# A Mamba-2 and short-convolution decode step on one core: VectorE's instructions go into written order through the scan

## Chip, core and metric

The kernel runs as one program on one core of a Trainium2 chip. The metric is the device time of one execution in microseconds. Three executions of the kernel before took 1029.29, 1029.47 and 1030.23 us, with a median of 1029.47 us. A further execution was taken with a profile; it took 1030.42 us, and the span of its instructions, from the first to the last, is 1028.60 us.

## The reference

One layer of a decoder trunk, for 256 prompt tokens and 8 sample sequences of 8 tokens each (320 columns in all), with a model width of 2048. All in float32:

```python
h = rmsnorm(x, norm_w)
proj = einsum('bld,de->ble', h, w_in)          # 2048 -> 13344 columns
z_s, xbc, dt_raw, z_c, b_c, c_c, v_c = split(proj)
xbc = silu(causal_dwconv(xbc, state, w4) + bias)      # x, B, C: width-4 convolution
xs, bm, cm = split(xbc)
dt = softplus(dt_raw + dt_bias);  a = -exp(a_log)
y_s, h_new = ssd_scan(xs, dt, a, bm, cm, d_skip, h0)  # 32 heads x 64, state 128, 4 groups
y_s = grouped_rmsnorm(y_s * silu(z_s), ssd_norm_w, 4)
conv_out = causal_dwconv(c_c * v_c, state2, w3)
y_c = b_c * conv_out * silu(z_c)
out = rmsnorm(x + concat(y_s, y_c) @ w_out, final_norm_w)
```

The scan works on chunks of 128 tokens. Inside a chunk, with the running sum `a_cum` of `dt * a`, it forms `decay = exp(min(a_cum[l] - a_cum[s], 0))` under a causal mask, `cb = C B^T`, and `y = (cb * decay) @ (x * dt)` for each head; between chunks it carries a state `h` of 64 x 128 for each head. The outputs are the two token groups' results and all new states.

## The kernel before

Everything is laid out with channels on the 128 partitions and the 320 tokens along the free dimension. The input projection is a loop over 104 weight tiles (`tiles`, made by `schedule()`, L82): each gives 128 output channels, as 16 steps over the contraction, each of three matmuls of 128 x 320. Three, because a float32 product is made out of high and low parts: `wh` and `wl` are the parts of the weights, `xh` and `xl` those of the input (`product`, L169). The order of the tiles is by group g = 0 to 3: `B`, `C`, (two short-convolution sets for g = 0), four `x`, four `z`, then one short-convolution set `sc`, `sv`, `sz`, `sb` (two for g = 3); nine more such sets follow. The output projection (16 tiles of two halves) comes last.

**Weights.** `load(i)` (L135) fetches a tile by two DMAs of 512 KB on SP's queue into three half buffers. `split(i)` (L163) cuts a tile into four quarters of 128 x 512: ScalarE casts the quarter to `wh` (L159), VectorE subtracts it from the raw weights and gets `wl` (L160). There are six buffers of a quarter for each, so the casts of quarters 2 and 3 of the next tile wait until TensorE has gone through quarters 0 and 1 of the tile in work. The loop (L793) writes, for tile i: load of i+2, split of i+1, the product of i, and then what is done with its result.

**What is done with a result.** `conv` (L500) for x, B and C: VectorE scales it out of PSUM into a padded tile, GpSimd puts in the old state and keeps the new one, ScalarE makes the first tap (L513), VectorE the other three (L515), ScalarE the SiLU (L518, L521). `short` (L745) is the like for the short convolution, with two taps on VectorE (L763). A `z` tile is scaled by VectorE (L821) and goes through SiLU on ScalarE. Tiles 0 to 5 (B0, C0 and the first short set) are made ahead of the loop, the first four of them in other PSUM tiles.

**The scan rides along.** `decays` (L414) makes the softplus, the running sums and the decay factors; `ssd_group` (L523) is the scan of one group. Both are Python generators, queued in `gens`; within each product, ahead of steps 5, 10 and 15 (`TICKS`), `advance(1)` runs the front one to its next `yield`. So the group's matmuls are spread among those of the projection, a part at a time. The group of z tiles starts its scan after tile z0 (L818); its first part stands at the first tick of z1, three parts to a tile. In the counting used below, part 1 has the transposes of B (L586), part 2 the product `cb` (L599), part 3 the samples' transposes of x (L610), part 5 the first chunk's transposes (L627) and out of them `xdt` and `xw` on VectorE (L629, L632), part 7 the state product `st` of the first chunk (L642, it reads `xw`), part 8 the second chunk's transposes, part 10 its `st`, part 11 the products with the old states, `py` and `up` (L656, L668). `rpart` (L553) makes one of five parts of the decay matrix: VectorE subtracts and clips (L570: four or eight instructions), ScalarE takes the exponential (L573), VectorE multiplies by the masked `cb` (L574). The updates of the old states are a product on GpSimd (L672) and an addition on VectorE (L679), and go out by DMAs on GpSimd's queue (L680).

**Who sets the order.** TensorE's instructions run as they are written (L182). The order on VectorE, ScalarE, GpSimd and SP is made by a planner when the program is built: it walks the written program with costs of its own, and an engine takes, at each planned instant, the first written one of the instructions that are then ready. On the chip each engine runs its list in that order, and an instruction whose input is late holds all that are behind it. Only in the tail, from L935, is VectorE's order the written one too. All small PSUM tiles of the scan share four buffers (`sm`, L111).

## Time and profile before

| | |
|---|---|
| median of three executions | 1029.47 us (1029.29 to 1030.23) |
| profiled execution | 1030.42 us, its span 1028.60 us |
| TensorE busy in the span | 1018.8 us (99%) |
| VectorE, ScalarE, GpSimd busy | 667.5, 492.6, 190.6 us |
| weight low parts on VectorE (L160) | 518 instructions, 365.4 us |
| weight casts on ScalarE (L159) | 518 instructions, 315.5 us |

The profile is of one execution. Its views give, for an engine and a line of the kernel, how long it was busy, and what ended the idle time ahead of an instruction; the timeline gives the start and the duration of single instructions, in us from the start of the span, and merges neighbours of the same line ("x4"). Instructions of one engine overlap at their ends, so the distance from one start to the next is shorter than the duration. A busy time of TensorE is taken from modelled ends, so its waits are seen best in the distance between the starts of two matmuls.

### The profile page before, as it was taken

What the parts mean: (1) busy time and instruction counts of PE and PEld (TensorE: products, weight loads), DVE (VectorE), ACT (ScalarE), POOL (GpSimd) and SP (SyncE); (2) the same over time, 40 slices, a digit from 0 to 9 for tenths busy, and PEclk for the clock granted to TensorE, in tenths of its full rate; (3) what the DMA queues carried; (4) which work ended last, traced back from release to release, by engine and by line L of the source; (5) the groups of instructions that cost most, each with busy time, mean ns of one, the idle gap of its engine ahead of it and who ended that gap; (6) DMA issues with size and microseconds to landing.
All of it is one profiled execution on the core that took longest, in us unless ns stands there. A gap on an engine that the chain in (4) does not pass through costs nothing.

```text
span 1028.6 us, 18694 instructions
## 1 busy us (share of the span) xinstructions
PE 1018.8 (99%) x7233; PEld 997.9 (97%) x7233; DVE 667.5 (65%) x1217; ACT 492.6 (48%) x891; POOL 190.6 (19%) x293
## 2 busy tenths in 40 slices
PE   9999999999999999999999999999999999999997
PEld 9999999999999989999999999999999999999996
DVE  7787758886878777886868555555556544444444
ACT  8456434573457445654445433433345544444450
POOL 0222034210622134213422101111111000000000
PEclk9999999999999999999999999999999999999999
DMA  9354475546473566447546444444445744444412
GB/s 370 118 158 164 143 256 176 177 152 216 165 230 119 193 225 205 144 160 264 180 149 244 163 144 148 160 144 146 154 152 155 256 153 145 150 156 146 148 38 103
DMA packets 63304, 176.62 MB, mean 172 GB/s; under 512 B 10496, under 2 KB 20352, under 8 KB 63088
## 3 DMA queue, kind: packets, MB, share of 16 engines
q1 hardware_dynamic: 59712, 164.98, 48.3%
q0 software_dynamic: 3072, 9.96, 2.7%
q8 instruction: 56, 0.92, 0.4%
q10 hardware_dynamic: 432, 0.49, 0.1%
q14 instruction: 32, 0.26, 0.1%
HBM read 162.83 MB, written 12.58 MB: 171 GB/s over the span
## 4 chain that ended last, share of the span: by engine, by line
PE 88%; DVE 5%; DMA 2%; issue 2%; POOL 1%; ACT 1%; DVEq 0%; POOLq 0%; SPq 0%; ACTq 0%
PE pj L176 20%; PE pj L175 20%; PE pj L177 20%; PE po L175 7%; PE po L176 7%; PE po L177 7%; PE pf L282 3%; DMA R<-acd 2%; POOL ht L672 1%; DVE wl L160 1%; PE pd L699 1%; DVE ht L679 1%; DVE R L570 1%; PE pt L926 1%; DVE R L574 1%
## 5 line engine op out<-in xcount | busy, mean ns | idle before, releaser
L160 DVE TENSOR_TENSOR wl<-wr,wh 128x512 fp32r<-128x512 f32 x518 | 365.4, 712 | 271.3 <-ACT wh L159 267.7
L159 ACT CAST wh<-wr 128x512 fp32r<-128x512 f32 x518 | 315.5, 618 | 393.1 <-PE pj L177 233.8
L175 PE MATMUL pj<-xh,wh 128*128 128x320 f32 x1600 | 501.8, 314 | 0.0
L176 PE MATMUL pj<-xh,wl 128*128 128x320 f32 x1600 | 494.8, 309 | 1.6 <-DVE wl L160 1.6
L177 PE MATMUL pj<-xl,wh 128*128 128x320 f32 x1600 | 494.3, 309 | 0.0
L175 PEld LDWEIGHTS pj<-xh,wh 128*128 128x128 f32 x1600 | 300.6, 188 | 6.0 <-issue 5.4
L176 PEld LDWEIGHTS pj<-xh,wl 128*128 128x128 f32 x1600 | 300.7, 188 | 5.2 <-DVE wl L160 3.0
L177 PEld LDWEIGHTS pj<-xl,wh 128*128 128x128 f32 x1600 | 300.6, 188 | 0.0
L175 PE MATMUL po<-ysh,wh 128*128 128x320 f32 (+1 forms) x256 | 78.3, 306 | 0.0
L176 PE MATMUL po<-ysh,wl 128*128 128x320 f32 (+1 forms) x256 | 78.3, 306 | 0.0
L177 PE MATMUL po<-ysl,wh 128*128 128x320 f32 (+1 forms) x256 | 78.3, 306 | 0.0
L175 PE MATMUL po<-ych,wh 128*128 128x320 f32 (+1 forms) x256 | 78.1, 305 | 0.0
L176 PE MATMUL po<-ych,wl 128*128 128x320 f32 (+1 forms) x256 | 78.1, 305 | 0.0
L177 PE MATMUL po<-ycl,wh 128*128 128x320 f32 (+1 forms) x256 | 78.0, 305 | 0.0
L177 PEld LDWEIGHTS po<-ysl,wh 128*128 128x128 f32 x256 | 48.1, 188 | 0.0
L175 PEld LDWEIGHTS po<-ysh,wh 128*128 128x128 f32 x256 | 48.1, 188 | 0.0
L176 PEld LDWEIGHTS po<-ysh,wl 128*128 128x128 f32 x256 | 48.1, 188 | 0.0
L176 PEld LDWEIGHTS po<-ych,wl 128*128 128x128 f32 x256 | 48.1, 188 | 0.0
L175 PEld LDWEIGHTS po<-ych,wh 128*128 128x128 f32 x256 | 48.0, 188 | 0.0
L177 PEld LDWEIGHTS po<-ycl,wh 128*128 128x128 f32 x256 | 48.0, 188 | 0.0
L902 POOL TENSOR_TENSOR acco<-acco,sqo 128x320 f32<-128x320 f32 x13 | 11.5, 881 | 186.7 <-ACT sqo L898 186.7
L515 DVE SCALAR_TENSOR_TENSOR cv<-pad,vec,cv 128x344 f32<-128x344 f32 x72 | 40.7, 570 | 2.7 <-ACT cv L513 1.6
(254 smaller groups left out, 899.4 us busy)
## 6 DMA issues: line engine op xcount, KB each, us to landing
wr<-in_w_in SPq DMA_DIRECT2D x200, 512.0 KB, 3.5
wr<-in_w_out SPq DMA_DIRECT2D x59, 512.0 KB, 3.7
ht<-in_h SPq DMA_DIRECT2D x32, 256.0 KB, 5.0
out_hs<-ht POOLq DMA_DIRECT2D x32, 256.0 KB, 3.0
R<-acd SPq DMA_DIRECT2D x20, 256.0 KB, 6.3
xw<-in_xw SPq DMA_DIRECT2D x6, 848.0 KB, 10.7
wk<-in_w_out SPq DMA_DIRECT2D x5, 512.0 KB, 6.6
resp<-in_xp SPq DMA_DIRECT2D x1, 2048.0 KB, 9.6
```

The source lines that it names most:

```text
L159: S.copy(h, r)
L160: V.tensor_sub(l, r, h.bitcast(F32))
L175: PE.matmul(ps, h, hi(k), start=start and k == 0, stop=False)
L176: PE.matmul(ps, l, hi(k), start=False, stop=False)
L177: PE.matmul(ps, h, lo(k), start=False, stop=stop and k == KT - 1)
L282: PE.matmul(ps0[i], w[:, i * P:(i + 1) * P], x[:, k, :], start=k == 0 and w is h and x is xh, stop=k == KT - 1 and w is l)
L515: V.scalar_tensor_tensor(out=a, in0=pad[:, k:k + CW], scalar=vec[:, w + k:w + k + 1], in1=a, op0=ALU.mult, op1=ALU.add)
L570: V.tensor_scalar(out=R[:, h, :], in0=R[:, h, :], scalar1=ac_tok[:, c, at:at + 1], scalar2=0.0, op0=ALU.subtract, op1=ALU.min)
L574: V.tensor_tensor(out=R, in0=R, in1=bc(CBm[:, o:o + n].rearrange("p (u l) -> p u l", u=1), [P, nh, n]), op=ALU.mult)
L672: GP.tensor_tensor(out=heads(ht, g), in0=heads(ht, g), in1=decay(b, g), op=ALU.mult)
L679: V.tensor_tensor(out=ht, in0=ht, in1=ups[j], op=ALU.add)
L902: GP.tensor_tensor(out=acc, in0=acc, in1=sq, op=ALU.add)
```

## The change

Four things, all in the order of work; no arithmetic is added or taken out.

1. From the product of tile 6 to the last tile of the scan, VectorE's instructions run as they are written (`manual_schedule` for DVE, closed when short set 6 is through).
2. In the written text, what VectorE makes out of a result of ScalarE or GpSimd is put behind one more `yield`: for the generators of the scan it then stands in the next part, for `conv` and `short` (now generators too, driven by `take` and `finish`) it stands behind the split of the next tile. The number of parts of the scan, and the part in which each matmul stands, are kept: other yields are taken out (`rpart` carries its own, and the wait loop of `decays` goes from 11 to 9).
3. B0 and C0 are no longer worked on ahead of tile 6, but after tile 6 and after tile 7.
4. In the group's norm the reciprocal goes into tile `b` in place of `v`, the tile that ScalarE's square root reads.

```diff
--- before.py
+++ after.py
@@ -423,6 +423,7 @@
         V.tensor_scalar(out=v, in0=v, scalar1=hv[:, 0:1], scalar2=None, op0=ALU.add)
         V.scalar_tensor_tensor(out=nv_, in0=v, scalar=-1.0, in1=v, op0=ALU.mult, op1=ALU.min)
         S.activation(u, nv, AF.Exp)
+        yield
         an = cp.tile([H, 1], F32, name="an")
         V.tensor_copy(an, u[:H, TQ:])
         u = u[:, :TQ]
@@ -461,9 +462,10 @@
         GP.tensor_copy(tot[:, :NB], win(ac, TP + NL - 1, (NL, NB)))
         GP.tensor_copy(tot[:, NB:], ac[:, TP - 1:TP])
         GP.dma_start(totd, tot)
+        yield
         V.tensor_tensor(out=wT[:, :T], in0=wx, in1=dtT[:, :T], op=ALU.mult)
         pad_samples(GP, stk)
-        for _ in range(11):
+        for _ in range(9):
             yield
         SP.dma_start(dec, bc(totd.rearrange("(u h) b -> u (h b)", u=1), [P, H * (NB + 1)]))
         p = sm("tr")
@@ -511,6 +513,7 @@
         a = tp.tile([P, CW], F32, name=f"cv{idx}", tag="cv")
         w = V_CW + 4 * idx
         S.mul(a, pad[:, 0:CW], vec[:, w:w + 1])
+        yield
         for k in range(1, 4):
             V.scalar_tensor_tensor(out=a, in0=pad[:, k:k + CW], scalar=vec[:, w + k:w + k + 1],
                                    in1=a, op0=ALU.mult, op1=ALU.add)
@@ -571,6 +574,7 @@
                                 scalar1=ac_tok[:, c, at:at + 1], scalar2=0.0,
                                 op0=ALU.subtract, op1=ALU.min)
             S.activation(R, R, AF.Exp)
+            yield
             V.tensor_tensor(out=R, in0=R,
                             in1=bc(CBm[:, o:o + n].rearrange("p (u l) -> p u l", u=1), [P, nh, n]),
                             op=ALU.mult)
@@ -590,9 +594,10 @@
         Bst = ssd.tile([P, 2, 2, P], F32R, name=f"Bst{g}", tag="Bst")
         for q in range(2):
             S.activation(Bst[:, q, 0, :], p[:, 2 * P:3 * P], AF.Copy, scale=mq[q])
+        yield
+        for q in range(2):
             V.scalar_tensor_tensor(out=Bst[:, q, 1, :], in0=p[:, 2 * P:3 * P], scalar=mq[q],
                                    in1=Bst[:, q, 0, :].bitcast(F32), op0=ALU.mult, op1=ALU.subtract)
-        yield
         p = sm(f"cb{g}")
         CBm = ssd.tile([P, T], F32, name=f"CBm{g}", tag="CBm")
         for c, (o, n, _) in enumerate(CH):
@@ -615,10 +620,9 @@
         xh_ = t5("xh2", F32R)
         S.activation(xh_, xw, AF.Copy, scale=sgn)
         xst = ssd.tile([P, 512], F32R, name=f"xst{g}", tag="xst")
+        yield
         V.scalar_tensor_tensor(out=xst, in0=xw, scalar=m1, in1=xh_.bitcast(F32), op0=ALU.mult, op1=ALU.add)
-        yield
-        rpart(0)
-        yield
+        yield from rpart(0)
 
         h1 = tl("h1")
         for c in range(2):
@@ -633,8 +637,9 @@
                             in1=perhead(w_tok[:, c, hs]), op=ALU.mult)
             yield
             if c == 0:
-                rpart(1)
-            yield
+                yield from rpart(1)
+            else:
+                yield
             if c == 0:
                 for b in range(4):
                     hload(2 * b)
@@ -642,13 +647,14 @@
             PE.matmul(p, Btok[:, c * P:(c + 1) * P], xw, start=True, stop=True)
             if c == 0:
                 S.copy(h1, p)
+                yield
             else:
                 hf = t5("hf")
                 GP.tensor_tensor(out=heads(hf, g), in0=heads(h1, g),
                                  in1=decay(NB, g), op=ALU.mult)
+                yield
                 V.tensor_tensor(out=hf, in0=hf, in1=p, op=ALU.add)
                 GP.dma_start(O["hp"][g], hf)
-            yield
 
         py = pss.tile([P, 512], F32, name=f"py{g}", tag="py", bufs=1)
         for q in range(2):
@@ -685,8 +691,7 @@
         V.tensor_tensor(out=xdt[2], in0=xdt[2], in1=py, op=ALU.add)
         yield
         for n_ in range(2, len(PARTS)):
-            rpart(n_)
-            yield
+            yield from rpart(n_)
             yield
         yield
         acc = ssd.tile([P, T], F32, name=f"acc{g}", tag="acc")
@@ -727,11 +732,11 @@
         V.tensor_scalar(out=v, in0=p[:, :T], scalar1=1.0 / (4 * P), scalar2=EPS,
                         op0=ALU.mult, op1=ALU.add)
         S.activation(a, v, AF.Sqrt)
-        V.reciprocal(v, v)
-        yield
-        V.tensor_tensor(out=v, in0=v, in1=a, op=ALU.mult)
-        V.scalar_tensor_tensor(out=b, in0=v, scalar=-0.5, in1=a, op0=ALU.mult, op1=ALU.mult)
-        V.scalar_tensor_tensor(out=b, in0=b, scalar=1.5, in1=v, op0=ALU.add, op1=ALU.mult)
+        V.reciprocal(b, v)
+        yield
+        V.tensor_tensor(out=b, in0=b, in1=a, op=ALU.mult)
+        V.scalar_tensor_tensor(out=v, in0=b, scalar=-0.5, in1=a, op0=ALU.mult, op1=ALU.mult)
+        V.scalar_tensor_tensor(out=b, in0=v, scalar=1.5, in1=b, op0=ALU.add, op1=ALU.mult)
         yield
         for j in range(4):
             ct = 4 * g + j
@@ -759,10 +764,11 @@
             a = tp.tile([P, SC], F32, name=f"sa{j}", tag="cv")
             w = V_SW + 3 * j
             S.mul(a, pad[:, 0:SC], vec[:, w:w + 1])
+            held["a"] = a
+            yield
             for k in range(1, 3):
                 V.scalar_tensor_tensor(out=a, in0=pad[:, k:k + SC], scalar=vec[:, w + k:w + k + 1],
                                        in1=a, op0=ALU.mult, op1=ALU.add)
-            held["a"] = a
         elif kind == "sz":
             a = held.pop("a")
             z = tp.tile([P, T], F32, name=f"sz{j}", tag="sz")
@@ -783,6 +789,7 @@
             V.tensor_tensor(out=y, in0=ps, in1=z, op=ALU.mult)
             if j >= NE:
                 S.copy(ych[:, j, :], y)
+                yield
                 V.tensor_sub(ycl[:, j, :], y, ych[:, j, :].bitcast(F32))
                 GP.tensor_copy(ycs[:, j, :], y[:, TP:])
 
@@ -790,41 +797,72 @@
     gens.append(decays())
     group = {}
 
-    for i in [*range(2, NFIRST + NAHEAD), 0, 1, *range(NFIRST + NAHEAD, nin)]:
+    def result(i, ps):
+
+        nonlocal zs
         kind, idx = tiles[i]
-        if i < NFIRST:
-            ps = ps0[i]
-        elif i in ahead:
-            ps = ahead.pop(i)
-        else:
-            load(i + 2)
-            split(i + 1)
-            ps = inproj(i)
         if kind in "BC":
             t = ssd.tile([P, T + P], F32, name=f"{kind}{idx}", tag=kind, bufs=2)
-            conv(ps, ((16 if kind == "B" else 20) + idx, i), t)
+            group[kind] = t
+            yield from conv(ps, ((16 if kind == "B" else 20) + idx, i), t)
             if kind == "B":
                 pad_samples(GP, t)
-            group[kind] = t
         elif kind == "x":
             t = ssd.tile([P, T + P], F32, name=f"x{idx}", tag="xs", bufs=6)
-            conv(ps, (idx, i), t)
+            group.setdefault("x", []).append(t)
+            yield from conv(ps, (idx, i), t)
             pad_samples(GP, t)
-            group.setdefault("x", []).append(t)
         elif kind == "z":
             if idx % 4 == 0:
-                advance(1000)
                 zs = []
                 gens.append(ssd_group(idx // 4, group["B"], group["C"], group["x"], zs))
-                group = {}
+                group.clear()
             z = ssd.tile([P, T], F32, name=f"z{idx}", tag="z", bufs=4)
             V.tensor_tensor(out=z, in0=ps, in1=rb, op=ALU.mult)
             S.activation(z, z, AF.Silu)
             zs.append(z)
         else:
-            short(kind, idx, ps)
+            yield from short(kind, idx, ps)
+
+    zs = None
+    late = []
+
+    def finish():
+        while late:
+            for _ in late.pop(0):
+                pass
+
+    def take(i, ps):
+        if tiles[i][0] == "z" and tiles[i][1] % 4 == 0:
+            advance(1000)
+        gen = result(i, ps)
+        if next(gen, late) is not late:
+            late.append(gen)
+
+    written = ExitStack()
+    for i in range(2, NFIRST + NAHEAD):
+        take(i, ps0[i] if i < NFIRST else ahead.pop(i))
+        finish()
+    first = [0, 1]
+    for i in range(NFIRST + NAHEAD, nin):
+        kind, idx = tiles[i]
+        load(i + 2)
+        split(i + 1)
+        finish()
+        if i == NFIRST + NAHEAD:
+
+            written.enter_context(tc.manual_schedule(engines={mybir.EngineType.DVE}))
+        ps = inproj(i)
+        take(i, ps)
+        if first:
+            finish()
+            n = first.pop(0)
+            take(n, ps0[n])
+        if kind[0] == "s":
             if idx == NE - 1 and kind == "sb":
+                finish()
                 advance(1000)
+                written.close()
                 sst_.close()
                 fp = ctx.enter_context(tc.tile_pool(name="fin", bufs=1, reuse_waits="tile"))
                 ych = fp.tile([P, NSH, T], F32R, name="ych")
@@ -835,6 +873,7 @@
                     S.copy(ych[:, n, :], early[:, n, :])
                     V.tensor_sub(ycl[:, n, :], early[:, n, :], ych[:, n, :].bitcast(F32))
                 GP.dma_start(O["cs"], cso)
+    finish()
     GP.dma_start(O["ss"], sso)
 
 
```

## The prediction

> **What bounds the kernel now.** I read the page's busy times first, then the waits of TensorE's weight loads (PEld), then the timeline around the longest of them.

> ```profile
> span 1028.6 us, 18694 instructions
> PE 1018.8 (99%) x7233; PEld 997.9 (97%) x7233; DVE 667.5 (65%) x1217; ACT 492.6 (48%) x891; POOL 190.6 (19%) x293
> ```
> ```profile
> PEld pj L176 <- DVE wl L160: 3.0, 5, 0.8
> ```
> ```profile
> 227.00:337.00 110.00, 109.59 (x791) 105.13 (x790) 85.92 (x162) 57.74 (x104) 32.10 (x46) 1.00 0.55 184
> ```

> TensorE is the bound. All that another order on VectorE can win is the time in which TensorE waits for VectorE's `wl` in the scan: five waits, 3.0 us, 0.29% of the run. The last row is the second group's 110 us (columns: length, then busy us of PE, PEld, DVE, ACT and POOL, the granted clock, the DMA share): the clock is full, and a group's 42 parts (14 tiles of three) are 2.6 us apart. About 0.2% (2.06 us) is what a measurement of this kernel can tell from no change. So the change has to keep over two thirds of those 3.0 us to be seen as faster.

> ```profile
> 170.33 0.31 PE L175 MATMUL pj<-xh,wh 128*128 128x320 f32 x1
> 171.18 0.41 PE L176 MATMUL pj<-xh,wl 128*128 128x320 f32 x1 [0.55 <-DVE wl L160]
> ```
> ```profile
> 166.78 0.69 DVE L679 TENSOR_TENSOR ht<-ht,up 128x512 f32<-128x512 f32 x1 [0.52 <-POOL ht L672]
> ...
> 170.44 1.29 DVE L160 TENSOR_TENSOR wl<-wr,wh 128x512 fp32r<-128x512 f32 x2
> ```
> ```profile
> 165.69 4.11 POOL L672 TENSOR_TENSOR ht<-ht,dec 128x512 f32<-128x512 f32 x4
> ```

> The reader is to see the cause in these rows: the planner put four state additions (L679) ahead of a `wl`; GpSimd takes 4.11 us for their four factors, each addition waits for its own, and the `wl` behind them comes at 170.44, its matmul 0.85 us after the one before it.

> **What the change removes.** In written order those additions stand two and three parts behind GpSimd's products, and the `wl` of the next tile stand ahead of them. The wait in that place goes in every group, four of the five; the fifth is of the same kind, a `wl` behind scan work, and I count it in: -3.0 us, and no more can be won. Nothing is late next in that place: GpSimd's 4.11 us end before the second part behind, 5.2 us on, and the next use of the additions, the PSUM for the second four `up`, is five parts behind the first. The later additions move `out_hs` on GpSimd's queue, and with it the release of the buffers into which SP's queue loads the next `R`; these are used six parts after the second four `up`. The loads on SP's queue keep their parts. The reciprocal (L730) no longer waits for the square root; no matmul of the scan reads its result. These edits I put at 0, covered by parts of the group in which TensorE needs nothing of VectorE.

> **What it adds: VectorE stops where it could have gone on.** Before a group's `xst` (part 4) stand, in written order, the four `wl` of the next tile, and the last of them waits for TensorE's own progress. What follows in VectorE's queue is, one behind the other: `xst`, eight subtractions of `rpart(0)`, [ScalarE's exponential], the product with `cb`, `xdt`, `xw`. TensorE's `st` in part 7 needs that `xw`. Before, the planner had made the whole `rpart(0)` a tile of x earlier. The rows of the first group:

> ```profile
> 126.96 0.62 ACT L159 CAST wh<-wr 128x512 fp32r<-128x512 f32 x1 [1.15 <-PE pj L177]
> 129.15 0.62 ACT L159 CAST wh<-wr 128x512 fp32r<-128x512 f32 x1 [1.57 <-PE pj L177]
> ```
> ```profile
> 91.59 1.31 DVE L570 TENSOR_SCALAR R<-R,ac_tok 128x64 f32<-128x64 f32 x7
> 124.72 0.75 DVE L618 SCALAR_TENSOR_TENSOR xst<-xw,con,xh 128x512 fp32r<-128x512 f32 x1
> 127.62 0.69 DVE L160 TENSOR_TENSOR wl<-wr,wh 128x512 fp32r<-128x512 f32 x1 [0.94 <-ACT wh L159]
> 128.23 0.69 DVE L629 TENSOR_TENSOR xdt<-xt,dt_tok 128x512 f32<-128x512 f32 x1
> 128.84 0.68 DVE L632 TENSOR_TENSOR xw<-xt,w_tok 128x512 f32<-128x512 f32 x1
> ```
> ```profile
> 150.46 1.28 ACT L562 ACT_TABLE_LOAD   x1 [6.20 <-DMA out_hp<-hf]
> 151.75 0.63 ACT L562 ACTIVATE CE<-R 128x512 f32<-128x512 f32 x1
> 165.95 1.28 ACT L770 ACT_TABLE_LOAD   x1
> 172.16 0.47 ACT L770 ACTIVATE sz<-sz 128x320 f32<-128x320 f32 x1 [4.93 <-DVE sz L769]
> ```
> ```profile
> 132.87 1.02 PE L642 MATMUL st<-xw,Btok 128*128 128x512 f32 x2
> ```

> The last `wl` of tile z3 starts at 127.62, since its cast is let go by TensorE at 126.96 and so is the same under the change. A 128x512 instruction takes the engine 0.61 us from start to start (128.23 to 128.84). `xst` then starts at 128.23 and takes 0.75 at the most; seven subtractions take 1.31, eight 1.5: they end at about 130.4. The exponential is 0.63. ScalarE's last function was the SiLU of z1, so it loads a table first, 1.28 us. The rows at 165.95 and 172.16 show that such a load runs ahead of the data that its function waits for, as far as ScalarE's own list lets it. Two ends, then. If the load is through by 130.4: exponential to 131.1, product 131.7, `xdt` 132.3, `xw` to 133.0, and with 0.05 to reach TensorE (ScalarE's end at 127.58 to VectorE's start at 127.62 is 0.04) 133.1, 0.25 us after 132.87. If the cast at 129.15, which is ready before the exponential and so stands ahead of it in a list made by readiness, comes first: cast to 129.77, load to 131.07, exponential to 131.7, product 132.3, `xdt` 132.95, `xw` to 133.64, at TensorE 133.7: a wait of 0.82 us. I take 0.82, because that cast is ready 1.2 us before the subtractions are done. Four groups: +3.3 us (bounds +1.0 and +3.3).

> [...]

> **A second new wait, at `up`.** The addition that ends `hf` (L649) moves from part 10 to part 11, behind a `wl` that waits for TensorE, and its PSUM buffer is one of the four that `up` of part 11 takes.

> ```profile
> 144.29 0.69 DVE L160 TENSOR_TENSOR wl<-wr,wh 128x512 fp32r<-128x512 f32 x1 [1.26 <-ACT wh L159]
> ```
> ```profile
> 145.35 0.74 PE L668 MATMUL up<-xst,Bst 32*128 32x512 f32 x8
> ```

> The addition can start at 144.29 + 0.61 = 144.90 and ends at 145.59; the fourth `up` begins at most 0.28 us (three eighths of 0.74) behind 145.35. With the 0.05 that is a wait of 0 to 0.29 us for each group; I take the middle, 0.15: +0.6 us (0 to 1.2). Behind the waiting addition on VectorE only part 13 is queued, and `out_hp` on GpSimd's queue goes 3 us later, which nobody waits for.

> **The start of the region.** B0 and C0 move behind tiles 6 and 7; their GpSimd copies and ScalarE's taps and SiLUs go with them. Now a SiLU of B0 lies between the two exponentials of `decays`, so another table load. VectorE's chain in tile 7, behind the last `wl` of tile 8: three taps of B0, parts 4 and 5 of `decays`, an exponential, `wT`, the scaling of `sv`, its taps, the scaling of C0, then the first `wl` of tile 9.

> ```profile
> 50.01 2.53 DVE L515 SCALAR_TENSOR_TENSOR cv<-pad,vec,cv 128x344 f32<-128x344 f32 x5 [0.72 <-ACT cv L513]
> 62.55 0.96 DVE L447 SCALAR_TENSOR_TENSOR stk<-v,q 32x80 f32<-32x80 f32 x4
> 64.14 0.37 DVE L450 TENSOR_SCALAR la<-stk,an 32x320 f32<-32x320 f32 x1
> 64.55 0.81 DVE L453 TENSOR_TENSOR_SCAN ac<-seg,la 32x320 f32<-32x320 f32 x1
> 65.29 0.79 DVE L456 TENSOR_TENSOR_SCAN wx<-la,ges 32x320 f32<-32x320 f32 x1
> 66.69 0.49 DVE L464 TENSOR_TENSOR stk<-wx,stk 32x320 f32<-32x320 f32 x1
> 67.21 0.42 DVE L754 TENSOR_TENSOR pad<-pj,c 128x256 f32<-128x256 f32 x1
> 67.56 0.21 DVE L756 TENSOR_TENSOR pad<-pj,c 128x64 f32<-128x64 f32 x1
> 68.48 1.17 DVE L763 SCALAR_TENSOR_TENSOR sa<-pad,vec,sa 128x336 f32<-128x336 f32 x2
> ```
> ```profile
> 61.78 0.62 ACT L159 CAST wh<-wr 128x512 fp32r<-128x512 f32 x1 [1.14 <-PE pj L177]
> 67.86 0.58 ACT L761 ACTIVATE sa<-pad,vec 128x336 f32<-128x336 f32 x1 [0.77 <-DVE pad L756]
> ```
> ```profile
> 72.28 0.31 PE L176 MATMUL pj<-xh,wl 128*128 128x320 f32 x1
> ```

> The last cast of tile 8 is let go by TensorE at 61.78, its `wl` is through by 63.05. Taps 1.5 (five in 2.53), parts 4 and 5 0.96 + 0.37 + 0.81 + 0.79 = 2.9: 67.5. The exponential, bounded by the 0.63 above: 68.1 if the table is in, 69.6 with the load and a cast in front of it. Then 0.49 + 0.63 + 0.7 (ScalarE's tap of `sv` and the ways to it and back) + 1.1 + 0.55 + 0.69 = 4.2: the first `wl` of tile 9 is there at 72.3 to 73.8, and TensorE wants it at 72.28. So 0 to 1.5 us; if the planner lets VectorE begin the region only after the `wl` of tile 7, I estimate as much again, 3 us. I take 1.4, since the list by readiness again has the cast and the load in front.

> **The sum**, against the profiled execution's own 1030.42 us (1.82 over its span, 0.95 over the median): -3.0 + 3.3 + 0.6 + 1.4 = +2.3. On the median: 1031.8 us. The terms' bounds give -3.0 + 1.0 + 0 + 0 = -2.0 to -3.0 + 3.3 + 1.2 + 3.0 = +4.5, so 1027.5 to 1034.0 for this case alone.

> **Rivals.**
> (1) Faster: the skew works as a whole. The place is `st` in part 7. If ScalarE's list has the exponential, and with it the load, ahead of the cast at 129.15, the wait there is at most 0.25, and the margin of the same size in my rounded durations may take it to 0; `up` and the start then wait 0 too. -3.0 us: 1026.5. It decides once all new waits together are under 0.9 us. For it: each new wait is under 1 us, and a load ahead of its data is in the rows. Against it: three places have to come out at their lower ends. Chance 0.25.
> (2) An exchange: the load is early (`st` waits 0.25), the start still 1.4, `up` 0.15: -3.0 + 1.0 + 1.4 + 0.6 = 0, 1029.5. Chance 0.17.
> (3) VectorE falls behind and weights come late.

> In a group's 110 us VectorE is busy 85.92 us, 78%. In written order it waits in each tile for two casts that TensorE lets go, and with five exponentials among the SiLUs of z, B and C it waits for table loads. The slack is 24 us for 14 or 15 tiles, 1.6 us each. If 2 us of waits are added in the tiles of B, C and x, `wl` come late there: two tiles by 1 us in each group, +8 us less the 3.0: 1034.5 or more. Against it: `wl` quarters are made about a tile ahead, 5 us early. Chance 0.08. [...]

> **How the numbers follow.** My forecast has the remaining 0.5; since two terms stand near their upper ends, 0.14 of it comes out within 0.2%. Faster by over 0.2%: 0.25. Within: 0.17 + 0.14 = 0.31. Slower: 0.36 + 0.08 = 0.44. The range goes from 1026.3 (the first rival, less the 0.2 us that the fastest run lies under the median) to 1034.8, just into the third rival.

> **What would show it.** In the new profile: no wait of PEld for `wl` at the four `sb` tiles (right); PE or PEld waiting at L642 for VectorE's `xw`, about 0.8 us, four times, with a table load in front of L573 there; a short wait at L668; a wait of over 1 us at the first `wl` of tile 9 near 72 us. If L642 shows no wait and the table load lies before the cast, my largest term is wrong. If waits for `wl` appear in x tiles, it is rival (3).

## The result, and the profile after

The changed kernel took 1044.26 us (median of four executions, 1042.31 to 1044.66), the kernel before 1029.78 us beside it. The ratio is 1.0136, with a 95% interval of 1.0124 to 1.0147: slower by 14.5 us, where 2.3 were forecast and the range ended 5.0 above. The profiled execution of the changed kernel took 1042.31 us. First its page, then the waits of TensorE's weight loads (in total, times, longest).

```profile
span 1040.2 us, 18681 instructions
PE 1023.4 (98%) x7233; PEld 999.9 (96%) x7233; DVE 668.2 (64%) x1217; ACT 511.9 (49%) x907; POOL 197.9 (19%) x293
```
```profile
PEld rg L730 <- POOL acc L723: 4.7, 4, 3.3
PEld st L647 <- PE pj L177: 4.2, 4, 1.1
...
PEld up L674 <- DVE ht L685: 3.1, 5, 0.8
...
PEld pj L176 <- DVE wl L160: 1.7, 1, 1.7
```

VectorE does the same work (668.2 us against 667.5). The waits for `wl` at the `sb` tiles are gone, as forecast; the one left is at the start. In their place TensorE waits at `rg`, `st` and `up`. To put a price on each place I compare the length of every tile in the two traces, from the start of its first matmul to that of the next tile's. The differences:

| place | forecast, us | measured, us |
|---|---|---|
| `wl` at the four `sb` tiles and at `sz2` | -3.0 | -2.6 (0.81, 0.67, 0.49, 0.67 won; `sz2`'s 0.34 not) |
| `st`, z3 to z15 | +3.3 | +4.2 (1.06 each) |
| `up`, the four `sc` tiles behind z3 to z15 | +0.6 | +1.1 (0.27 each) |
| start, tile 9 | +1.4 | +1.7 |
| end of the scan, tiles 67 and 68 | 0 | +4.7 (3.62 and 1.05) |
| `rg` in x6, x10, x14 (0.92, 0.35, 0.18), second `up` in the `sz` tiles, others | 0 | +2.3 |

They add up to 11.3 us; the spans differ by 11.6. Over half of the loss is in two rows that were priced at nothing.

**The last tile of the scan.** Tile 67 is `sb6`, and the rest of the fourth group is written at its end. VectorE and TensorE of the changed kernel there:

```profile
540.01 0.96 DVE L160 TENSOR_TENSOR wl<-wr,wh 128x512 fp32r<-128x512 f32 x1 [1.31 <-ACT wh L159]
541.23 0.89 DVE L160 TENSOR_TENSOR wl<-wr,wh 128x512 fp32r<-128x512 f32 x1 [0.26 <-ACT wh L159]
542.04 0.53 DVE L714 SCALAR_TENSOR_TENSOR y<-x,vec,pd 128x320 f32<-128x320 f32 x1
...
544.08 1.15 DVE L717 TENSOR_TENSOR z<-y,z 128x320 f32<-128x320 f32 x1
```
```profile
547.00 1.43 PE L730 MATMUL rg<-acc,ones 128*128 128x320 f32 x2 [3.00 <-POOL acc L723]
...
548.50 0.47 PE L176 MATMUL pj<-xh,wl 128*128 128x320 f32 x1
548.76 0.47 PE L177 MATMUL pj<-xl,wh 128*128 128x320 f32 x1
```

The same place in the kernel before (GpSimd's last sum, then `rg`), and GpSimd's last sum in the changed kernel:

```profile
531.39 0.88 POOL L718 TENSOR_TENSOR acc<-acc,sq 128x320 f32<-128x320 f32 x1 [0.58 <-ACT sq L717]
```
```profile
537.18 0.70 PE L725 MATMUL rg<-acc,ones 128*128 128x320 f32 x2
```
```profile
545.87 1.07 POOL L723 TENSOR_TENSOR acc<-acc,sq 128x320 f32<-128x320 f32 x1 [0.99 <-ACT sq L722]
```

In the kernel before, the sum was through 4.9 us ahead of `rg`. In the changed kernel the `y` of the last heads stands behind two `wl` quarters of the next tile, for whose casts VectorE waits 1.31 and 0.26 us: ScalarE has a table load and a SiLU (from 537.70 on) ahead of the first cast, and TensorE lets the second go at 540.58. `gy` (`z<-y,z` in the rows), its square and GpSimd's sum follow, and `rg` with all of TensorE's list behind it waits 3.00 us for that sum. Then the matmuls come 0.27 us apart instead of 0.15 until 550.05. The windows around it (columns as in the prediction, with GB/s as the last; the seventh number is the granted clock) show half the clock behind the idle time:

```profile
543.22:546.63 3.41, 0.78 (x6) 0.52 (x4) 3.01 (x5) 2.35 (x4) 1.89 (x2) 1.00 0.40 142
546.63:550.05 3.42, 3.05 (x9) 2.66 (x10) 1.55 (x2) 0.93 (x2) 0.81 (x2) 0.50 0.40 153
550.05:553.46 3.41, 3.41 (x25) 3.41 (x24) 2.64 (x5) 1.24 (x2) 0.00 (x0) 1.00 0.00 0
```

**`st`** is as the prediction had it, cast and table load ahead of the exponential (ScalarE, VectorE, TensorE):

```profile
130.87 0.62 ACT L159 CAST wh<-wr 128x512 fp32r<-128x512 f32 x1 [1.57 <-PE pj L177]
131.51 1.28 ACT L576 ACT_TABLE_LOAD   x1
132.80 0.63 ACT L576 ACTIVATE R<-R 128x512 f32<-128x512 f32 x1
```
```profile
133.54 0.69 DVE L578 TENSOR_TENSOR R<-R,CBm 128x512 f32<-128x512 f32 x1 [1.54 <-ACT R L576]
134.15 0.68 DVE L633 TENSOR_TENSOR xdt<-xt,dt_tok 128x512 f32<-128x512 f32 x1
134.75 0.68 DVE L636 TENSOR_TENSOR xw<-xt,w_tok 128x512 f32<-128x512 f32 x1
```
```profile
135.57 1.10 PE L647 MATMUL st<-xw,Btok 128*128 128x512 f32 x2 [0.82 <-DVE xw L636]
```

**`up`**: eight matmuls took 0.74 us before; the fourth of them now waits for `hf`'s addition (TensorE, then VectorE):

```profile
148.13 1.01 PE L674 MATMUL up<-xst,Bst 32*128 32x512 f32 x8
```
```profile
147.06 0.69 DVE L160 TENSOR_TENSOR wl<-wr,wh 128x512 fp32r<-128x512 f32 x1 [1.93 <-ACT wh L159]
147.67 0.68 DVE L656 TENSOR_TENSOR hf<-hf,st 128x512 f32<-128x512 f32 x1
```

**ScalarE in its own list.** The planner still orders ScalarE. It put the exponential of `CE` (L565) early, into tile `sv`; its buffer is one that `hf` held, so it waits for the store of `hf`, and the weight casts stand behind it. ScalarE, then VectorE:

```profile
155.17 1.28 ACT L565 ACT_TABLE_LOAD   x1 [4.26 <-DMA out_hp<-hf]
156.47 0.63 ACT L565 ACTIVATE CE<-R 128x512 f32<-128x512 f32 x1
157.00 2.72 ACT L159 CAST wh<-wr 128x512 fp32r<-128x512 f32 x5
```
```profile
157.64 2.59 DVE L160 TENSOR_TENSOR wl<-wr,wh 128x512 fp32r<-128x512 f32 x3 [4.10 <-ACT wh L159]
160.15 2.47 DVE L685 TENSOR_TENSOR ht<-ht,up 128x512 f32<-128x512 f32 x4
```

The same stop stands in the profile of before (6.20 us at 150.46), where VectorE's list had the four state additions ahead of the `wl` that waited:

```profile
150.01 2.47 DVE L679 TENSOR_TENSOR ht<-ht,up 128x512 f32<-128x512 f32 x4
```

In written order VectorE can't go round it: three `wl` wait 4.10 us, the four state additions come behind them, and the second four `up` wait for their PSUM.

### The profile page after: what moved, and what is told of

Its sections match the earlier page's. It is cut to its first block, busy times and chain, and to the rows that moved or that the text cites. A ratio compares the mean times of both kernels' runs of the same rounds, so it can differ in the third digit from the quotient of the medians.

```text
span 1040.2 us, 18681 instructions
## 1 busy us (share of the span) xinstructions
PE 1023.4 (98%) x7233; PEld 999.9 (96%) x7233; DVE 668.2 (64%) x1217; ACT 511.9 (49%) x907; POOL 197.9 (19%) x293
## 4 chain that ended last, share of the span: by engine, by line
PE 91%; DVE 5%; ACT 1%; issue 1%; DMA 1%; POOL 1%; DVEq 0%; ACTq 0%
PE pj L175 21%; PE pj L176 20%; PE pj L177 20%; PE po L175 7%; PE po L177 7%; PE po L176 7%; PE pf L282 3%; DVE wl L160 2%; DVE cv L518 1%; PE py L662 1%; PE st L647 1%; PE up L674 1%; PE pt L965 1%; POOL acc L723 1%; DMA wr<-in_w_in 1%
## 5 line engine op out<-in xcount | busy, mean ns | idle before, releaser
L160 DVE TENSOR_TENSOR wl<-wr,wh 128x512 fp32r<-128x512 f32 x518 | 371.5, 738 | 264.7 <-ACT wh L159 261.1
L159 ACT CAST wh<-wr 128x512 fp32r<-128x512 f32 x518 | 314.1, 618 | 397.3 <-PE pj L177 240.2
L175 PE MATMUL pj<-xh,wh 128*128 128x320 f32 x1600 | 502.8, 314 | 0.0
L176 PE MATMUL pj<-xh,wl 128*128 128x320 f32 x1600 | 495.3, 310 | 1.5 <-DVE wl L160 1.5
L177 PE MATMUL pj<-xl,wh 128*128 128x320 f32 x1600 | 494.9, 309 | 0.0
L175 PEld LDWEIGHTS pj<-xh,wh 128*128 128x128 f32 x1600 | 301.0, 188 | 6.1 <-issue 5.5
L176 PEld LDWEIGHTS pj<-xh,wl 128*128 128x128 f32 x1600 | 301.1, 188 | 4.3 <-issue 2.1
L177 PEld LDWEIGHTS pj<-xl,wh 128*128 128x128 f32 x1600 | 300.8, 188 | 0.0
L175 PE MATMUL po<-ysh,wh 128*128 128x320 f32 (+1 forms) x256 | 78.3, 306 | 0.0
L176 PE MATMUL po<-ysh,wl 128*128 128x320 f32 (+1 forms) x256 | 78.3, 306 | 0.0
L177 PE MATMUL po<-ysl,wh 128*128 128x320 f32 (+1 forms) x256 | 78.3, 306 | 0.0
L175 PE MATMUL po<-ych,wh 128*128 128x320 f32 (+1 forms) x256 | 78.1, 305 | 0.0
L176 PE MATMUL po<-ych,wl 128*128 128x320 f32 (+1 forms) x256 | 78.1, 305 | 0.0
L177 PE MATMUL po<-ycl,wh 128*128 128x320 f32 (+1 forms) x256 | 78.0, 305 | 0.0
L176 PEld LDWEIGHTS po<-ysh,wl 128*128 128x128 f32 x256 | 48.1, 188 | 0.0
L175 PEld LDWEIGHTS po<-ysh,wh 128*128 128x128 f32 x256 | 48.1, 188 | 0.0
L177 PEld LDWEIGHTS po<-ysl,wh 128*128 128x128 f32 x256 | 48.1, 188 | 0.0
L176 PEld LDWEIGHTS po<-ych,wl 128*128 128x128 f32 x256 | 48.1, 188 | 0.0
L175 PEld LDWEIGHTS po<-ych,wh 128*128 128x128 f32 x256 | 48.0, 188 | 0.0
L177 PEld LDWEIGHTS po<-ycl,wh 128*128 128x128 f32 x256 | 48.0, 187 | 0.0
L678 POOL TENSOR_TENSOR ht<-ht,dec 128x512 f32<-128x512 f32 x32 | 38.9, 1242 | 29.9 <-PE py L662 29.8
```

Source lines behind the costliest of these rows:

```text
L159: S.copy(h, r)
L160: V.tensor_sub(l, r, h.bitcast(F32))
L175: PE.matmul(ps, h, hi(k), start=start and k == 0, stop=False)
L176: PE.matmul(ps, l, hi(k), start=False, stop=False)
L177: PE.matmul(ps, h, lo(k), start=False, stop=stop and k == KT - 1)
L678: GP.tensor_tensor(out=heads(ht, g), in0=heads(ht, g), in1=decay(b, g), op=ALU.mult)
```

## Experiments

**Theory**: in written order all that stands behind a `wl` whose cast TensorE or a stopped ScalarE holds is late by that wait; the losses are separate places of this one kind. **Rivals**: the moves themselves make the work late, in whatever order; or the losses hide one another, so that mending one shows the next.

### One part undone at a time

Four edits of the changed kernel. In the first, the product with `cb` of the first `rpart` goes behind the first chunk's `xdt` and `xw`:

```diff
-        yield from rpart(0)
+        r0 = rpart(0)
+        next(r0)
+        yield
...
+            for _ in r0:
+                pass
             yield
```

> The changed kernel, with one thing moved: the product of rpart(0) with cb (L578) stands behind xdt and xw of the first chunk on VectorE, not ahead of them. Theory (what holds TensorE at the state product st is only that xw stands behind ScalarE's late exponential in VectorE's written order): the four waits at L647 go, each of 1.06 us in the start-to-start distances, so 4.2 us less than the changed kernel: span near 1036.0 us, and no wait of TensorE for xw. Rival (TensorE is held there by VectorE's lateness as a whole): the waits shrink by less than half or come back one part later, and the span stays above 1038.

1040.13 us (1038.37 to 1040.65), ratio 1.0093 (1.0076 to 1.0110). The four waits at L647 are gone; the 0.27 us at `up` stay. The second puts `hf`'s addition back into part 10:

```diff
-                yield
                 V.tensor_tensor(out=hf, in0=hf, in1=p, op=ALU.add)
                 GP.dma_start(O["hp"][g], hf)
+                yield
```

> The changed kernel, with the addition that ends hf put back into part 10. Theory (the fourth up waits for the PSUM that this addition reads): tiles sc of each group are 0.27 us shorter, 1.1 us in all, span near 1039.1. Rival (VectorE is late there anyway, or then waits for TensorE's st with wl queued behind it): sc tiles as long as in the changed kernel, span 1040 or more.

1045.43 us (1044.83 to 1045.76), ratio 1.0149 (1.0134 to 1.0165); `up` waits the same 0.27 us. The expectation missed: nothing else of VectorE's is written between parts 10 and 11, and the order of its 1217 instructions is the same in both traces. The third takes B0 and C0 ahead of the region again, the fourth closes the written order before tile `sz6`, so that the planner orders the end:

```diff
-    for i in range(2, NFIRST + NAHEAD):
+    for i in [*range(2, NFIRST + NAHEAD), 0, 1]:
...
-    first = [0, 1]
+    first = []
```
```diff
         kind, idx = tiles[i]
+        if (kind, idx) == ("sz", NE - 1):
+            finish()
+            written.close()
```

> The changed kernel, with B0 and C0 worked on ahead of tile 6 again. Theory (the late wl of tile 9 comes from B0's taps, C0's scaling and the table load between the two exponentials of decays, all in VectorE's chain of tile 7): the wait of 1.7 us in tile 9 goes, no other takes its place, span near 1038.5. Rival (the first convolutions had to move because VectorE's work ahead of tile 6 does not fit): a wait of 1 us or more in tiles 7 or 8 instead, span 1039.5 or more.

> The changed kernel, with VectorE's written order ended ahead of tile sz of the last short set in the scan, three tiles earlier. Theory (at the end of the scan the norm's product rg follows part 33 at once, and y and gy of the last heads stand in written order behind the wl of the next tile): the 3.0 us wait at L730 goes, and with it the stretch at half clock behind it: tiles sb6 and sc7 3.6 and 1.05 us shorter, span near 1035.5, clock 0.999. Rival (GpSimd's and ScalarE's chain of squares and additions is the late one): the wait stays above 2 us.

1040.29 us (1039.43 to 1043.02), ratio 1.0105 (1.0090 to 1.0120), and 1039.23 us (1038.13 to 1040.06), ratio 1.0089 (1.0074 to 1.0104). In the third the wait at tile 9 is gone; in the fourth tiles 67 and 68 have before's lengths, and the windows there show the full clock:

```profile
546.00:551.00 5.00, 5.00 (x36) 5.00 (x35) 5.00 (x7) 2.67 (x5) 0.46 (x1) 1.00 0.55 202
```

The profiled executions of the first and the third, spans 1038.6 and 1041.2 us, were the slowest of their four and missed the expected 1036.0 and 1038.5: what stands in the last row of the table above, 2.3 us there, is about 4.7 and 5.1 us in them, by the lengths of the tiles. It varies from run to run, and the place itself is read from the tiles.

### The order or the moves

In one kernel the parts stay where the change put them, but `manual_schedule` for VectorE is left out; in the other it is put around the same tiles of the kernel before, and nothing is moved.

```diff
-            written.enter_context(tc.manual_schedule(engines={mybir.EngineType.DVE}))
+            pass
```

> The changed kernel with every part where the change put it, but VectorE's order left to the planner as before. Theory: the loss comes from the written order (VectorE cannot go around an instruction that waits), so without it the waits at st, up and rg and the long wait at the end of the scan go, and the waits for wl behind the four state additions come back (about 3 us in all): 1029 to 1032 us. Rival: the moved parts themselves cost (the work stands a part later and TensorE needs it where it did): then the waits at st, up and rg and the 3.6 us in the last tile of the scan stay, and the time is 1038 us or more.

> The kernel before, with only the written order on VectorE through the scan; no part is moved. Theory: without the moves every instruction of VectorE that follows a ScalarE or GpSimd result in the same part stands and waits for it with the weights behind it, so waits of TensorE for wl appear in all stages: over 1050 us. Rival: the moved parts are what costs, and the order alone is cheap: under 1040 us.

1030.24 us (1029.08 to 1031.64), ratio 1.0006 (0.9996 to 1.0016), and 1075.70 us (1074.57 to 1079.10), ratio 1.0453 (1.0435 to 1.0471). The moves cost nothing where VectorE's list is the planner's, so the first rival falls; the waits for `wl` came back in part (1.6 us of the 3.0). The order alone costs 46 us, and the moves win 31 of them back. The waits of the kernel with the order alone (for `wl` six long ones, not many in all stages; the mean granted clock of its profiled execution is 0.983 besides, where the kernel before has 0.997 to 0.999):

```profile
PEld pj L176 <- DVE wl L160: 20.2, 6, 3.9
PEld rg L725 <- POOL acc L718: 8.7, 4, 4.4
PEld up L668 <- DVE ht L679: 6.6, 12, 0.8
...
PEld st L642 <- PE pj L177: 4.2, 4, 1.1
```

### The held `wl` out of the way

The third and fourth quarter of the next tile are those whose casts TensorE lets go. Here they are split not ahead of the tile but at its first and second tick, behind the part that is written there:

```diff
+        rest = [2, 3] if i + 1 in halves else []
...
+        def tick():
+            advance(1)
+            if rest:
+                splits[i + 1].append(split_quarter(i + 1, rest.pop(0)))
...
-        split(i + 1)
+        if i > NFIRST + NAHEAD and i + 1 < nin:
+            load(i + 1)
+            halves.add(i + 1)
+            splits[i + 1] = [split_quarter(i + 1, q) for q in range(2)]
+        else:
+            split(i + 1)
```

> The changed kernel, with the third and fourth wl of the next tile (those whose casts wait for TensorE's progress) written at the two later parts inside the tile, and not ahead of it; the order stays written. Theory: what stood behind those two wl (xw, the last subtraction of decay factors, hf's addition, the last heads' y) comes up to 2.6 us earlier, so st waits at most 0.2 us, up 0, rg 0 and the last tile of the scan under 1 us with no half clock: 1031 to 1035 us. Rival: the wl themselves come late instead, behind the scan's parts (two tiles in each group by 1 us): waits for wl of over 5 us in all, 1040 us or more.

1031.82 us (1031.04 to 1033.59), ratio 1.0024 (1.0015 to 1.0034): 12.4 of the 14.5 us by this alone. No wait at `st` or `rg` in x tiles is left, `up`'s tiles have before's length, and two longer tiles remain: the start, 2.81 us, and 1.16 at the end, with a mean granted clock of 0.999. VectorE of this kernel in the stretch that was shown for `st`:

```profile
129.65 1.38 DVE L582 TENSOR_SCALAR R<-R,ac_tok 128x64 f32<-128x64 f32 x8
130.95 0.68 DVE L160 TENSOR_TENSOR wl<-wr,wh 128x512 fp32r<-128x512 f32 x1
132.87 0.69 DVE L587 TENSOR_TENSOR R<-R,CBm 128x512 f32<-128x512 f32 x1 [1.24 <-ACT R L585]
133.48 0.68 DVE L642 TENSOR_TENSOR xdt<-xt,dt_tok 128x512 f32<-128x512 f32 x1
134.08 0.68 DVE L645 TENSOR_TENSOR xw<-xt,w_tok 128x512 f32<-128x512 f32 x1
```

The wait for the exponential is now partly filled with a `wl`, and `xw` starts at 134.08 instead of 134.75. `hf`'s addition starts at 145.56 instead of 147.67, and the eight `up` take 0.74 us again:

```profile
145.56 0.69 DVE L665 TENSOR_TENSOR hf<-hf,st 128x512 f32<-128x512 f32 x1
```
```profile
148.59 0.74 PE L683 MATMUL up<-xst,Bst 32*128 32x512 f32 x8
```

### ScalarE's stop

`hf` gets a buffer in the ring of `xdt` and `h1`, so that no later tile of the twelve-buffer ring waits for its store.

```diff
-                hf = t5("hf")
+                hf = tl("hf")
```

> The changed kernel, with hf in the ring of xdt and h1 (a buffer of its own there) and not in the twelve-buffer ring, so that no later tile of that ring waits for hf to be stored. Theory: the exponential of CE that ScalarE has first in its list behind hf's store no longer stands before the weight casts; the waits at sz, B and rg that differ from run to run shrink by 1 to 2 us: 1040 to 1043 us, and the four waits of ScalarE at L565 for out_hp are gone. Rival: the next buffer of the ring, held by a state's store, makes the same wait: no change (1042 to 1045 us).

1039.79 us (1038.23 to 1040.81), ratio 1.0098 (1.0083 to 1.0113), more than expected. No wait for `out_hp` is left in ScalarE's list. ScalarE and VectorE of this kernel, in the stretch that was shown from 155.17 on:

```profile
146.98 1.28 ACT L565 ACT_TABLE_LOAD   x1
151.89 0.63 ACT L565 ACTIVATE CE<-R 128x512 f32<-128x512 f32 x1 [3.62 <-DMA R<-acd]
```
```profile
156.73 2.47 DVE L685 TENSOR_TENSOR ht<-ht,up 128x512 f32<-128x512 f32 x4
```

ScalarE now stops for the load of `R` instead, but the exponential starts 4.6 us earlier and the additions 3.4 us earlier.

### All together, and one left out

The edits at `st`, at the start, at the end and for `hf` in one kernel; then with the late split of quarters 3 and 4 too; then that without `hf`'s edit.

> The changed kernel with the four single edits together: the product with cb behind xw at the group's first part, B0 and C0 ahead of the region again, the written order closed before the last tiles of the scan, hf in a buffer of its own. If the losses are separate terms they add up: of the profile's eleven us the waits at st (4.2), at the start (1.7), at the end of the scan (4.7) and those that vary (1 to 2) go, up's 1.1 stays, and the 2.6 won at the sb tiles stays won: 1028 us (1027 to 1029.5). Rival: they hide one another (what is removed at one place is waited for at the next, since the weights are made at most a tile ahead): 1031 us or more.

> As the kernel with the four edits together, and the third and fourth wl of the next tile written inside the tile. If the separate terms hold, up's 1.1 us goes as well, and nothing of the written order is left that TensorE waits for: 1027 us (1026 to 1028), faster than the kernel before by over 0.2%. Rival: the order by hand gives no more than the planner's: 1029 to 1031 us.

> As the kernel with all five edits, but hf again in the twelve-buffer ring. If ScalarE's stop at L565 for hf's store costs on its own, 0.5 to 1.5 us more than with hf in its own buffer; if it only costs where VectorE is already held by the two late wl, the same time within 0.3 us.

1029.04 us (1028.75 to 1029.47), ratio 0.9994 (0.9985 to 1.0003); 1027.74 us (1027.33 to 1028.36), ratio 0.9984 (0.9975 to 0.9992); 1027.79 us (1027.39 to 1028.46), ratio 0.9984 (0.9975 to 0.9993). The second rival falls: in the first of them only `up`'s 0.27 us is left of the losses, and nothing else shows up. The last two beat both kernels, the one before by about 0.16%, short of the 0.2% that was expected. In the trace of the second all five waits for `wl` are won, 2.97 us against the 3.0 of the prediction, and no tile of the scan is longer than before. With the late split `hf`'s buffer makes no difference.

The first of these three, whose times spread by 0.7 us, serves as the base for leaving out one edit at a time:

> The kernel with the four edits together, less the one at st. By the trace's terms the four waits at st come back, 4.2 us: 1033.2 us. By the single edits: 4.1, the same, so here both agree; a smaller number would mean that another edit covers it.

> The kernel with the four edits together, less the one that puts B0 and C0 ahead of the region. By the trace's term only the wait for the first wl of tile 9 comes back, 1.7 us: 1030.7 us. By the single edit 4.0 us: 1033.0, and the extra time must then be seen at a place behind the start.

> The kernel with the four edits together, less the one that closes the written order before the last tiles of the scan. By the trace's term 3.6 us of idle time in the last tile of the scan, and where TensorE gets half its clock behind it 1.1 us or more in the tile after it: 1032.7 to 1034.5 us. By the single edit 5.0 us: 1034.0.

> The kernel with the four edits together, less hf's buffer of its own. By the trace's term ScalarE stops again at L565 for hf's store and the second four up wait for the state additions: 0.5 to 2 us, 1029.5 to 1031.0, with a wider spread from run to run. By the single edit 4.5 us: 1033.5.

| left out | us | over 1029.04 | in its trace, at its place |
|---|---|---|---|
| `st` | 1033.41 | +4.4 | 1.06 in each of z3, z7, z11, z15 |
| start | 1030.64 | +1.6 | 1.72 in tile 9 |
| end of the scan | 1034.96 (of three; a fourth took 2029.56, and no trace of it was kept) | +5.9 | 3.62 and 2.41 in tiles 67 and 68; mean granted clock 0.995, 0.998 in the base |
| `hf`'s buffer | 1032.38 | +3.3 | `rg` in x6, x10, x14; `up` in `sz2`, `sz4`; B3, x4, `sc6` |

The sum is 15.2 us, and the changed kernel stands 15.2 over the same base. With each time taken against the kernel before that ran beside it, the sum is 16.2 and the changed kernel 15.0 over the base. So these four are the loss, and they add up to within about 1 us. That the single edits above gave 17.6 together I put down to the term of ScalarE's stop, which varies from run to run (in the profiled execution of the changed kernel it is 2.3 us, and that execution is 2 us under the median). Two expectations missed: `hf`'s 3.3 us lies between the two values given, and the end's 5.9 is over both, with tile 68 longer by 2.41 us where it was 1.05 in the changed kernel. With the start's edit left out only the trace's 1.7 us come back, not the 4.0 of the single edit.

### From which idle time on the clock is halved

Twelve idle times of TensorE are made in the tiles behind the scan, in the kernel with the order closed early (`IDLE` gives 2 to 9 instructions for every second tile from 71 to 93):

```diff
+        if i in IDLE:
+            d = sm(f"d{i}")
+            PE.matmul(d[:, :P], bc(ones, [P, P]), ident, start=True, stop=True)
+            e = tp.tile([P, T], F32, name=f"e{i}", tag="cv")
+            V.tensor_copy(e[:, :P], d[:, :P])
+            for _ in range(IDLE[i]):
+                V.tensor_scalar(out=e[:, :P], in0=e[:, :P], scalar1=1.0, scalar2=None, op0=ALU.mult)
+            PE.matmul(d[:, P:2 * P], bc(ones, [P, P]), e[:, :P], start=True, stop=True)
+            V.tensor_copy(e[:, :P], d[:, P:2 * P])
```

> The changed kernel with its order closed before the last tiles of the scan, and twelve artificial idle times of TensorE in the tiles behind the scan (a small matmul, a chain of 2 to 9 VectorE instructions on its result, a small matmul that reads it), estimated at 1.5 to 4 us. It asks from which idle time on TensorE is given half its clock. If a length alone decides, every idle time above some value between 1.7 us (no half clock in the changed kernel) and 3.0 us (half clock there) has 3.4 us of half clock behind it and none below. If it also depends on where the idle time falls in a fixed period, idle times of the same length differ in it.

One execution, 1095.70 us. Seven of the twelve idle times have half the clock behind them, the shortest of 1.95 us; five have not, the longest of 3.46 us. TensorE's rows, then windows of 3.41 us, laid on the times at which the clock changed in this run:

```profile
575.13 0.49 PE L868 MATMUL d<-e,ones 128*128 128x128 f32 x2 [1.95 <-DVE e L867]
...
594.65 0.49 PE L868 MATMUL d<-e,ones 128*128 128x128 f32 x2 [3.20 <-DVE e L867]
...
612.45 0.49 PE L868 MATMUL d<-e,ones 128*128 128x128 f32 x2 [3.00 <-DVE e L867]
...
669.82 0.49 PE L868 MATMUL d<-e,ones 128*128 128x128 f32 x2 [3.46 <-DVE e L867]
```
```profile
572.50:575.91 3.41, 1.46 (x12) 1.27 (x11) 2.39 (x8) 1.00 (x2) 0.24 (x1) 1.00 0.57 190
575.91:579.33 3.42, 3.42 (x15) 3.42 (x14) 0.16 (x2) 0.62 (x1) 0.00 (x0) 0.50 0.31 121
592.98:596.39 3.41, 1.74 (x12) 1.74 (x13) 1.84 (x7) 0.00 (x0) 0.20 (x1) 1.00 0.42 154
596.39:599.81 3.42, 3.42 (x25) 3.42 (x24) 1.09 (x2) 1.24 (x2) 0.00 (x0) 1.00 0.00 0
...
664.66:668.07 3.41, 1.69 (x13) 1.50 (x11) 2.50 (x6) 1.56 (x3) 0.20 (x1) 1.00 0.42 154
668.07:671.49 3.42, 1.67 (x12) 1.68 (x13) 1.88 (x8) 0.00 (x0) 0.20 (x1) 1.00 0.42 153
```

Where TensorE was busy for 1.46 us of a window, the next one has a clock of 0.50; with 1.74 us it has 1.00. The 3.00 us before 612.45 have half the clock behind them (1.01 us busy in the window from 610.05, a clock of 0.50 in the one from 613.46), and the longer 3.20 us before 594.65, which fall on two windows, have not. The 3.46 us before 669.82 fall on two windows with 1.69 and 1.67 us busy; the second of them has a clock of 1.00, and the next window at 0.50 is that from 688.55. So in this run a length alone doesn't decide.

## Why the prediction was wrong

The direction was right, and the four places of the sum came out near their terms; the size was wrong because two more places were not in the sum.

- **What it removes**: right. -2.6 in the changed kernel, -2.97 where nothing else holds VectorE, against -3.0.
- **`st`**: right in its cause, row for row. The tile is 1.06 longer. Of the 0.24 us between, 0.16 are the ways between the engines, which I had from one row: the exponential ends at 132.80 + 0.63 = 133.43 and VectorE starts at 133.54, 0.11 later and not 0.04; `xw` ends at 135.43 and TensorE starts at 135.57, 0.14 later and not 0.05. The other 0.08 stay open. +4.2 instead of +3.3 (+4.4 by the edit left out). The function starts at 132.80, right behind the load (131.51 + 1.28 = 132.79), as at 151.75 in the kernel before (150.46 + 1.28 = 151.74).
- **`up`**: 0.27 us instead of 0.15, inside the bounds, but not for the reason given. The move from part 10 to part 11 does nothing: without it VectorE's order is the same and the 0.27 us stay. It is the written order itself that puts `hf`'s addition behind the `wl`; the late split lets it go 2.1 us earlier and takes the 0.27 away, though that edit moves other work too.
- **The start**: 1.7 against 1.4; right.
- **The step that failed**: "These edits I put at 0, covered by parts of the group in which TensorE needs nothing of VectorE", and in it "no matmul of the scan reads its result". That holds for the reciprocal, but I went through the edits and not through what the order does to instructions that weren't edited. `rg` reads GpSimd's sum, which reads VectorE's `gy`, and at the end of the scan `rg` is written with no part between: nothing covers it. 3.0 us of waiting and half the clock behind it, 4.7 us in the profiled execution and 5.9 by the edit left out.
- **The second failure**: rival (3), "VectorE falls behind and weights come late", got 0.08, with casts that TensorE lets go and table loads for its waits. The wait that counts stood in a row that the prediction quotes, ScalarE's 6.20 us for `out_hp` at 150.46; I read it for the table load, and not as a stop in front of the weight casts, and wrote of `out_hp` that it goes later on GpSimd's queue, "which nobody waits for". ScalarE waits for it. In the kernel before that cost nothing, since VectorE's planned order went round it: with the moved parts and the planner's order ScalarE waits 20.7 us there in all, and no tile of x is longer. In the changed kernel it costs 3.3 us by the edit left out and 4.5 by the single edit, for the most part through `rg` in x tiles and the second `up`, and little through late `wl`. That `hf`'s buffer is the cause is shown by these two edits; how the delay travels to an `rg` several tiles on was not followed row by row.

## What to carry to other kernels

When an engine's order is fixed by hand, price every wait that it can no longer go round, not only the instructions that the diff moves: list the instructions that another engine gates, and ask for each what stands behind it and who reads that. Look at the end of a region for itself, where the parts that cover a wait in its middle are missing. And write gated work (here the two late quarters) at the point where its gate opens: that one edit gave back 12.4 of 14.5 us.

## What the runs showed of the hardware

- Ahead of the seven windows at 0.50 TensorE was busy for 0.28, 0.33, 0.56, 0.68, 0.92, 1.01 and 1.46 us, ahead of the one in the changed kernel for 0.78.
- Five windows with 1.69, 1.74, 1.76, 1.98 and 2.01 us busy were each followed by one at 1.00.

These are thirteen windows of two traces. What happens between 1.46 and 1.69 us, and in other kernels, they don't show.

In the trace of the changed kernel the matmuls of the projection come 0.267 us apart in the stretch at 0.50 (548.76 to 549.83) and 0.147 at 1.00 (550.08 to 551.99). By an estimate from these distances, 3.41 us at 0.50 start about 13 of them in place of 23, which costs about 1.5 us where TensorE is busy throughout.
